# A hybrid transformer block on one core: head norms taken from unscaled products, and six steps of the first head group placed anew

## The chip, the core and the metric

The kernel runs on one core of a Trainium2 chip. The core has five engines with an instruction queue each: PE multiplies matrices and transposes, DVE (vector), ACT (scalar functions) and POOL (general) do element work, and SP issues most of the DMAs. The metric is the device time of one execution in microseconds (us), smaller being better. A difference is told as faster or slower only where it is over 0.2%.

## The reference

One layer of a trunk for 512 tokens of width 1024. A norm and one input projection of 3590 columns give the queries, keys and values of three groups of attention heads of width 64: A (4 heads, two softmax maps a head that are subtracted), B (6 heads, with a running sum of log forget gates) and C (6 heads). Their outputs go through one output projection, then come a gated MLP with a convolution over three tokens and a gated per-layer input. What matters here:

```python
def rms_norm(x, g):
    y = x * lax.rsqrt(jnp.mean(x * x, axis=-1, keepdims=True) + EPS)
    return y * g

hn = rms_norm(h, ln_mix[i])
z = hn @ w_in[i]
(q1, q2, k1, k2, va, qf, kf, vf, fg, qc, kc, vc) = jnp.split(z, IN_SPLITS, axis=-1)
q1 = rms_norm(split_heads(q1, H_DIFF), g[0])      # and so every q and k, per head of 64 columns
```

So a query or key is normed twice: its token's row of 1024 by the layer norm, then its 64 columns by the head norm.

## The kernel before

All matrix products are made of three passes over operands that are split into a high and a low part (`mm3`: high by high, high by low, low by high). The token tiles have 128 tokens, t = 0 to 3. The layer norm's gain is put on the transposed input; its factor per token, a column of `rstd`, isn't multiplied in before the projection, so the products z are unscaled. `token_stats` (L227) makes for a tile the sum of squares on ACT and then three operations of one column on POOL: mean plus EPS (L233), its power -0.5, which is the factor itself (L234), and its square over 64 (L235). The same helper serves the MLP's norm and the last norm, where the fourth column has no reader.

`qk_sums` (L404) squares a tile's 256 query and key columns on ACT, sums each head's 64 squares on DVE, scales the four sums by the fourth column and adds EPS (on DVE for the first pair of heads, on POOL for all others) and raises them to -0.5 on POOL. `qk_scale` (L416) multiplies z by the token's factor and by the head's; its result is called zn. The values are scaled by the token's factor in `in_unit` (L470).

The projection runs pair of heads by pair of heads: A0, A0b (the second map's queries and keys of A0, with the forget gates), A1, A1b, B0 to C2. A part's four token tiles are four slots, each of eight groups of three products (j = 0 to 7), one for each 128 rows of the weight. Slots 0 to 3 hold the first part, written out in `first_products` (L329), where the orders of ACT and DVE are fixed as written; slots 4 to 7 are A0b, 8 to 11 A1, 12 to 15 A1b, 16 to 19 B0, and so on.

The attention of a pair is cut into steps that are laid between the groups. The table `T` (L751) gives for each step its slot and the first group j behind which it may run; `run` (L731) takes one step behind each group, in order of these starts, each step list in its turn, and what is left runs behind the slot's last group. The order on PE is fixed by this. On ACT, DVE, POOL and SP the order of this part is set by a planner that goes by its own estimates of time and by the program's order; `EARLY` (L766) moves some steps forward in it. The steps that matter here:

- `A0a`, `A0b`, `A1a`, `A1b` (`qk_cols`, L505): four transposes of zn for the queries, then four for the keys, each with splits on ACT and DVE and copies of half tiles on POOL, because a head's high and low parts lie in the two halves of the partitions. The queries' tile is named q_p, the keys' k_p. Each takes a bank of PSUM that something before must have left.
- `fc` (`forget_cumsum`, L518), three steps: gates on ACT and DVE; four transposes (pf), a scan on DVE and a DMA of the sums to memory; four transposes back (pq).
- `A0s01`, `A0s02`, `A0s11`, `A0s12` (`scores`, L594): head 0 and head 1, query blocks 0 and 1, or 2 and 3. Each block has two maps; each is two products, a biased minimum on DVE, an exponential on ACT and a reciprocal; POOL scales the second (named with a b, such as A_3b_e) and DVE adds the two. The scores use two PSUM banks in turn. The bias table of a head is made on POOL at its first step, in one of three buffers that `fc` uses too.
- `A0p0`, `A0p1` (`prob_cols`, L618): the transposes of the probabilities, pt and ptc. `A0v0`, `A0v1` (`values`, L646): products of these with the values, po.

Of the kernel before, what the change touches and what calls it, by code (L numbers as in the profile page):

```python
# [12 lines left out]
ALU = mybir.AluOpType  # L13
AX = mybir.AxisListType

P = 128
# [4 lines left out]
HD = 64  # L21
# [3 lines left out]
EPS = 1e-6  # L25
# [56 lines left out]
def kernel(ctx: ExitStack, tc: tile.TileContext, x, xt0, xt, pt_in, small, g_ffn_in, bias_c,  # L82
# [9 lines left out]
    nc = tc.nc  # L92
# [23 lines left out]
    pe, act, dve, pool, sp = (Engine(e) for e in (nc.tensor, nc.scalar, nc.vector, nc.gpsimd, nc.sync))  # L116
# [21 lines left out]
    rstd = cp.tile([P, NT, 4], F32, tag="rstd", name="rstd")  # L138
# [87 lines left out]

    def token_stats(t, src, junk, last=False):  # L227

        r = rstd[:, t, :]
        ins = act.activation(junk, src, AF.Square, accum_out=r[:, 0:1])  # L230
        if last:
            tc.keep_in_program_order(ins)
        nc.gpsimd.tensor_scalar(r[:, 1:2], r[:, 0:1], 1.0 / D, EPS, ALU.mult, ALU.add)  # L233
        nc.gpsimd.tensor_tensor(out=r[:, 2:3], in0=r[:, 1:2], in1=nhalf[:, 0:1], op=ALU.pow)  # L234
        nc.gpsimd.tensor_scalar(r[:, 3:4], r[:, 2:3], r[:, 2:3], 1.0 / HD, ALU.mult, ALU.mult)  # L235

    def split_cols(src, t, g, name, gain=None, tag="t"):

# [69 lines left out]
    for b in range(2):  # L308
        for i in range(2):
            c = HALF[1 - i]  # L310
# [12 lines left out]
    def stats(t):  # L323
        token_stats(t, h[:, t, :], ap.tile([P, D], BF16, tag="e3", bufs=2, name=f"n1_sq{t}"))
        done("n", t)
# [78 lines left out]
    def qk_sums(z, t, name):  # L404
        if name == "A0":
            sq = ap.tile([P, 3 * P], F32, tag="e2", bufs=2, name=f"{name}_sq{t}")[:, : 2 * P]
        else:
            sq = ap.tile([P, 2 * P], F32, tag="sq", bufs=1, name=f"{name}_sq{t}")
        act.activation(sq, z[:, 0 : 2 * P], AF.Square)
        rs = ap.tile([P, 8], F32, tag="rs", bufs=3, name=f"{name}_rs{t}")  # L410
        dve.tensor_reduce(out=rs[:, 0:4], in_=sq.rearrange("p (g c) -> p g c", c=HD), axis=AX.X, op=ALU.add)
        (dve if name in ("A0", "A0b") else pool).tensor_scalar(rs[:, 0:4], rs[:, 0:4], rstd[:, t, 3:4], EPS, ALU.mult, ALU.add)
        pool.tensor_tensor(out=rs[:, 4:8], in0=rs[:, 0:4], in1=nhalf[:, 0:4], op=ALU.pow)
        return rs

    def qk_scale(z, zn, t, rs):  # L416
        dve.scalar_tensor_tensor(zn[:, t, :].rearrange("p (g c) -> p g c", c=HD),
                                       z[:, 0 : 2 * P].rearrange("p (g c) -> p g c", c=HD), rstd[:, t, 2:3],
                                       rs[:, 4:8].unsqueeze(2).broadcast_to([P, 4, HD]), ALU.mult, ALU.mult)

    def feature_cols(zn, j, name):
# [48 lines left out]
    def in_unit(pr, part, n, t, ws, prefetch):  # L470
# [11 lines left out]
        def evac(sums=True, rest=True):  # L482
            if not rest:
                return qk_sums(z, t, name)
            if part == 0:
                v = V[pr]
                vh = bass.AP(v.tensor, v[:, t, :].offset, [v.ap[0], [192, 2], [1, HD]])
                zv = z[:, 2 * P : 3 * P].rearrange("p (g c) -> p g c", c=HD)
                act.activation(vh, zv, AF.Copy, scale=rstd[:, t, 2:3])
                dve.scalar_tensor_tensor(v[:, t, HD : HD + P].rearrange("p (g c) -> p g c", c=HD), zv,  # L490
                                               rstd[:, t, 2:3], f32(vh), ALU.mult, ALU.subtract)
            elif n > 2 * P:
                dve.scalar_tensor_tensor(fg[:, t, 0:6], z[:, 2 * P : 2 * P + 6], rstd[:, t, 2:3], fgb,
                                               ALU.mult, ALU.add)
            return qk_sums(z, t, name) if sums else None

        def evac_done(rs=None):
            qk_scale(z, ZN[pr, part], t, rs or evac())
            done("in", pr, part, t)
# [231 lines left out]
    def run(fill, todo):  # L731
# [17 lines left out]
                pass  # L749

    T = {  # L751
# [112 lines left out]
    for j, (pr, part, *_) in enumerate(PARTS[1:], 1):  # L864
# [7 lines left out]
        for t in range(NT):  # L872
# [3 lines left out]
            if slot >= 37:  # L876
                c = slice((slot - 37) * P, (slot - 36) * P)
# [41 lines left out]
    def ffn_norm(t):  # L919

        token_stats(t, h[:, t, :], mtmp(BF16, 2, f"n2_sq{t}"))
        HN[t] = []
        for g in range(2):
            c = slice(g * S, (g + 1) * S)
            hn = mtmp(F32, 1, f"n2_hn{t}_{g}")
            dve.scalar_tensor_tensor(hn, h[:, t, c], rstd[:, t, 2:3], g_ffn[:, c], ALU.mult, ALU.mult)
            HN[t].append(hn)
# [540 lines left out]
    def first(f, g, a):  # L1468
        def do():
            c = g * NF + f  # L1470
            if a == 0:
                U[c] = bank("zs"[g], f"u{c}")
            cs = slice(a * H, (a + 1) * H)
            for k in range(KD):
                mm3(U[c][:, cs], *first_w[f][1](g, k), Th[k // 4][:, k % 4, cs], Tl[k // 4][:, k % 4, cs], k == 0, k == KD - 1)

        if a == 0:
            us[f, g] = Slot("zs"[g])
        return pe_task(24, do, [first_w[f][0][g], first_w[f][0][2]], FORM if a else (), [us[f, g]] if a == 0 else (), [us[f, g]] if a else ())
# [52 lines left out]
    for f in range(2):  # L1532
        p = [[first(f, g, 1)] for g in range(2)]
# [65 lines left out]
    def stats3(t):  # L1599
        def do():  # L1600
            token_stats(t, h[:, t, :], mtmp(BF16, 2, f"n3_sq{t}"))

        STATS[t] = Task("do", [("act", 1.15)], do, list(H_ADDS.values()), [Slot("conv")])
# [64 lines left out]
    t = 0.0  # L1668
# [122 lines left out]
```

## Time and profile before

| What | Value |
|---|---|
| median of three runs | 725.68 us (725.09 to 725.84) |
| profiled execution, its time | 725.56 us |
| its span | 723.8 us |
| PE busy, products | 706.4 us (98%) |
| PE busy, weight loads | 631.9 us (87%) |
| DVE busy | 536.2 us (74%) |
| ACT busy | 391.8 us (54%) |
| POOL busy | 220.2 us (30%) |
| chain of work that ended last | PE 78%, DVE 10%, DMA 3%, ACT 3%, POOL 2% |

The profile names an instruction by line, engine and operation, then output and inputs. A row of the timeline has its start, its length in us and how many were merged into it, and in brackets how long the engine had been idle before it and what ended that. A row of waits has their total, number and longest. A row of windows gives the stretch, its length, PE's busy time with the number of products, the granted clock as a share of the full one, and the DMA's share and GB/s. A row for one tile gives the count and the shortest, median and longest of an instruction in ns, with the first and last start. Products overlap in a pipeline, so that the length of one is more than the time from one start to the next. The profiler gives nearly all helper instructions the line L108, so one goes by the names of tiles.

### The profile page before, as it was taken

What the parts mean: (1) busy time and instruction counts of PE and PEld (TensorE: products, weight loads), DVE (VectorE), ACT (ScalarE), POOL (GpSimd) and SP (SyncE); (2) the same over time, 40 slices, a digit from 0 to 9 for tenths busy, and PEclk for the clock granted to TensorE, in tenths of its full rate; (3) what the DMA queues carried; (4) which work ended last, traced back from release to release, by engine and by line L of the source; (5) the groups of instructions that cost most, each with busy time, mean ns of one, the idle gap of its engine ahead of it and who ended that gap; (6) DMA issues with size and microseconds to landing.
All of it is one profiled execution on the core that took longest, in us unless ns stands there. A gap on an engine that the chain in (4) does not pass through costs nothing.

```text
span 723.8 us, 11826 instructions
## 1 busy us (share of the span) xinstructions
PE 706.4 (98%) x4182; PEld 631.9 (87%) x4182; DVE 536.2 (74%) x1085; ACT 391.8 (54%) x739; POOL 220.2 (30%) x339
## 2 busy tenths in 40 slices
PE   9898999999999999999999999999999999999997
PEld 8897989988999887889889899988988888999886
DVE  8578787887878854857776998897857677677542
ACT  6646775865766663556354363645434445435721
POOL 4675675766665640200200505100010000000400
PEclk9999999999999999999999999999999999999999
DMA  9444446628414425563844463995595332742441
GB/s 328 176 138 115 123 118 164 204 66 265 131 57 140 146 49 169 161 227 61 190 106 137 96 226 83 242 200 182 167 236 158 94 91 88 234 143 82 156 130 56
DMA packets 43383, 107.35 MB, mean 148 GB/s; under 512 B 4886, under 2 KB 6550, under 8 KB 43324
## 3 DMA queue, kind: packets, MB, share of 16 engines
q1 hardware_dynamic: 38028, 89.51, 38.6%
q0 software_dynamic: 5008, 16.78, 12.8%
q8 instruction: 33, 0.54, 0.3%
q10 hardware_dynamic: 288, 0.30, 0.1%
q14 instruction: 26, 0.21, 0.1%
HBM read 98.31 MB, written 25.18 MB: 171 GB/s over the span
## 4 chain that ended last, share of the span: by engine, by line
PE 78%; DVE 10%; DMA 3%; ACT 3%; POOL 2%; issue 2%; SPq 0%; POOLq 0%; ACTq 0%; DVEq 0%
PE u L108 28%; PE dn_X L108 8%; PE C_z L108 6%; PE pg L108 6%; PE wo L108 5%; PE B_z L108 4%; PE dn_Y L108 4%; PE dn_Z L108 2%; PE A_z L108 2%; DVE w_lo L108 1%; DMA h<-in_x_dram 1%; PE pp L108 1%; PE C_s L108 1%; DVE A_e L108 1%; PE sX L108 1%
## 5 line engine op out<-in xcount | busy, mean ns | idle before, releaser
L108 PE MATMUL u<-Tl,w_hi 128*128 128x512 f32 (+1 forms) x352 | 131.9, 375 | 0.8 <-DVE Tl L108 0.8
L108 PE MATMUL u<-Th,w_hi 128*128 128x512 f32 (+1 forms) x352 | 131.9, 375 | 0.1
L108 PE MATMUL u<-Th,w_lo 128*128 128x512 f32 (+1 forms) x352 | 131.6, 374 | 0.0
L108 ACT CAST w_hi<-w_raw 128x768 fp32r<-128x768 f32 (+1 forms) x116 | 88.6, 786 | 73.2 <-PE u L108 32.4
L108 DVE TENSOR_TENSOR w_lo<-w_raw,w_hi 128x768 fp32r<-128x768 f32 (+1 forms) x116 | 106.5, 933 | 27.5 <-ACT w_hi L108 27.4
L108 DVE SCALAR_TENSOR_TENSOR c<-u,cols,c 128x511 f32<-128x511 f32 x80 | 59.6, 747 | 26.4 <-ACT c L108 25.2
L108 PEld LDWEIGHTS u<-Tl,w_hi 128*128 128x128 f32 x352 | 66.0, 188 | 13.9 <-DVE Tl L108 1.2
L108 PEld LDWEIGHTS u<-Th,w_lo 128*128 128x128 f32 x352 | 66.0, 188 | 13.2
L108 PEld LDWEIGHTS u<-Th,w_hi 128*128 128x128 f32 x352 | 66.0, 188 | 13.1 <-ACT pps L108 0.5
L233 POOL TENSOR_SCALAR rstd<-rstd 128x1 f32<-128x1 f32 x12 | 2.6, 216 | 155.2 <-ACT n_sq L108 154.8
L108 ACT ACTIVATE c<-u,cols 128x512 f32<-128x512 f32 x40 | 31.0, 776 | 29.1 <-PE u L108 29.1
L108 PE MATMUL dn_X<-w_hi,g_ah 128*128 128x256 f32 x144 | 40.6, 282 | 0.4 <-ACT c L108 0.4
L108 PE MATMUL dn_X<-w_hi,g_al 128*128 128x256 f32 x144 | 40.4, 281 | 0.0
L108 PE MATMUL dn_X<-w_lo,g_ah 128*128 128x256 f32 x144 | 40.4, 280 | 0.0
L108 POOL TENSOR_TENSOR w_raw<-w_raw,w_raw 128x768 f32<-128x768 f32 x8 | 15.5, 1938 | 67.1 <-DVE w_lo L108 56.4
L108 PE MATMUL B_z<-B_h,Th 128*128 128x384 f32 x96 | 34.6, 360 | 0.6 <-DVE B_zn L108 0.6
L108 POOL TENSOR_SCALAR tok<-c 128x1 f32<-128x1 f32 x15 | 7.7, 510 | 90.1 <-DVE c L108 90.1
L108 PE MATMUL C_z<-C_h,Th 128*128 128x384 f32 x96 | 34.3, 357 | 0.0
L108 PE MATMUL C_z<-C_h,Tl 128*128 128x384 f32 x96 | 32.3, 337 | 0.0
L108 PE MATMUL B_z<-B_h,Tl 128*128 128x384 f32 x96 | 32.3, 337 | 0.0
L108 PE MATMUL C_z<-C_l,Th 128*128 128x384 f32 x96 | 32.3, 336 | 0.0
L108 PE MATMUL B_z<-B_l,Th 128*128 128x384 f32 x96 | 32.3, 336 | 0.0
(488 smaller groups left out, 2107.0 us busy)
## 6 DMA issues: line engine op xcount, KB each, us to landing
w_raw<-in_w_up_dram SPq DMA_DIRECT2D x44, 384.0 KB, 4.7
w_raw<-in_w_down_dram SPq DMA_DIRECT2D x20, 384.0 KB, 3.6
dsum<-in_w_dsum_dram SPq DMA_DIRECT2D x8, 768.0 KB, 7.0
w_raw<-dsum SPq DMA_DIRECT2D x16, 384.0 KB, 3.7
w_raw<-in_w_up_dram SPq DMA_DIRECT2D x20, 256.0 KB, 4.7
B_r<-in_w_in_dram SPq DMA_DIRECT2D x12, 384.0 KB, 3.4
C_r<-in_w_in_dram SPq DMA_DIRECT2D x12, 384.0 KB, 4.1
wo_r<-in_w_out_dram SPq DMA_DIRECT2D x16, 256.0 KB, 3.0
```

Of the source, the lines that this page charges most:

```text
L108: ins = getattr(self.eng, op)(*a, **k)
L233: nc.gpsimd.tensor_scalar(r[:, 1:2], r[:, 0:1], 1.0 / D, EPS, ALU.mult, ALU.add)
```

## The change

In `token_stats` the fourth column becomes 64 EPS times the mean plus EPS, made from L233's result ahead of the power. In `qk_sums` this is added to the unscaled sum of squares, in place of a product and an addition of EPS. In `qk_scale` the product with the token's factor becomes one with the constant 8, the root of 64. The normed result is the same, since the token's factor cancels: z r / sqrt(r² S / 64 + EPS) = 8 z / sqrt(S + 64 EPS / r²). Six entries of `T` change: A0a goes from group 2 to group 6 of slot 6, fc from 0 to 5 of slot 11, A0s11 and A0s12 from 0 and 1 to 2 and 4 of slot 13, A0v1 from 7 and A1a from 4 to 2 of slot 16.

```diff
@@ token_stats
         nc.gpsimd.tensor_scalar(r[:, 1:2], r[:, 0:1], 1.0 / D, EPS, ALU.mult, ALU.add)
+        nc.gpsimd.tensor_scalar(r[:, 3:4], r[:, 1:2], EPS * HD, None, ALU.mult)
         nc.gpsimd.tensor_tensor(out=r[:, 2:3], in0=r[:, 1:2], in1=nhalf[:, 0:1], op=ALU.pow)
-        nc.gpsimd.tensor_scalar(r[:, 3:4], r[:, 2:3], r[:, 2:3], 1.0 / HD, ALU.mult, ALU.mult)
@@ qk_sums
-        (dve if name in ("A0", "A0b") else pool).tensor_scalar(rs[:, 0:4], rs[:, 0:4], rstd[:, t, 3:4], EPS, ALU.mult, ALU.add)
+        (dve if name in ("A0", "A0b") else pool).tensor_scalar(rs[:, 0:4], rs[:, 0:4], rstd[:, t, 3:4], None, ALU.add)
@@ qk_scale
-                                       z[:, 0 : 2 * P].rearrange("p (g c) -> p g c", c=HD), rstd[:, t, 2:3],
+                                       z[:, 0 : 2 * P].rearrange("p (g c) -> p g c", c=HD), HD ** 0.5,
@@ T
-        "A0a": (6, 2), "A0b": (9, 4), "fc": (11, 0), "A1a": (16, 4), "A1b": (17, 0), "A0s01": (10, 4),
-        "A0s02": (10, 5), "A0p0": (12, 3), "A0s11": (13, 0), "A0v0": (12, 5), "A0s12": (13, 1), "A0p1": (15, 5),
-        "A0v1": (16, 7), "A0n": (17, 0), "A1s01": (18, 2), "A1s02": (18, 5), "A1p0": (20, 5), "A1s11": (20, 6),
+        "A0a": (6, 6), "A0b": (9, 4), "fc": (11, 5), "A1a": (16, 2), "A1b": (17, 0), "A0s01": (10, 4),
+        "A0s02": (10, 5), "A0p0": (12, 3), "A0s11": (13, 2), "A0v0": (12, 5), "A0s12": (13, 4), "A0p1": (15, 5),
+        "A0v1": (16, 2), "A0n": (17, 0), "A1s01": (18, 2), "A1s02": (18, 5), "A1p0": (20, 5), "A1s11": (20, 6),
```

## The prediction

> **What bounds the kernel now.** I read the page's busy times first, then the list of what the matrix engine (PE) waited for, then its rows in order of time around each wait, then the rows of whoever ended the wait.
>
> ```profile
> span 723.8 us, 11826 instructions
> PE 706.4 (98%) x4182; PEld 631.9 (87%) x4182; DVE 536.2 (74%) x1085; ACT 391.8 (54%) x739; POOL 220.2 (30%) x339
> ```
>
> PE is busy for 706.4 of 723.8 us. Nothing in the diff takes a matmul away, so a gain can come only out of the 17.4 us of idle time or out of time at a lower clock. The waits by name:
>
> ```profile
> PE A_q_p L108 <- DVE A_zn L108: 1.9, 2, 1.0
> PE A_pt L108 <- DVE A_e L108: 1.2, 1, 1.2
> ...
> PE A1b_z L108 <- DVE A1b_zn L108: 1.0, 1, 1.0
> ...
> PE pq L108 <- DVE fs L108: 0.9, 1, 0.9
> ...
> PE A_k_p L108 <- DVE A0b_zn L108: 0.6, 1, 0.6
> ```
>
> These five are group A waits, 5.6 us in all, each close to a step that the diff moves. The first and the last are one place, the transposes of the first pair, and the clock falls just behind it (windows of PE, then their granted clock):
>
> ```profile
> 28.90:32.30 3.40, 1.03 (x6) 1.00 0.00 0
> 62.50:65.90 3.40, 2.15 (x19) 1.00 0.85 275
> ```
> ```profile
> 33.00:34.00 1.00, 1.00 (x7) 0.50 0.00 0
> ...
> 35.00:36.00 1.00, 1.00 (x7) 0.53 0.58 174
> 36.00:37.00 1.00, 1.00 (x10) 1.00 0.64 240
> ```
>
> PE worked 1.03 of 3.40 us, and about 3.4 us at half clock followed (0.50, back at 1.00 in the slice from 36). With 2.15 of 3.40 busy, at the A_pt wait, no slice drops.
>
> **A0a four groups later.** In slot 6 it stood behind three of eight groups of three products; it will stand behind seven.
>
> ```profile
> 21.57 0.28 PE L108 MATMUL A0b_z<-A0b_h,Th 128*128 128x262 f32 x1
> ...
> 28.40 0.28 PE L108 MATMUL A0b_z<-A0b_h,Tl 128*128 128x262 f32 x1
> 28.52 0.38 PE L108 MATMUL A_q_p<-ident,A_zn 128*128 128x128 f32 x2
> ...
> 31.10 0.33 PE L108 MATMUL A_q_p<-ident,A_zn 128*128 128x128 f32 x1 [0.95 <-DVE A_zn L108]
> ...
> 32.36 0.94 PE L108 MATMUL A_k_p<-ident,A_zn 128*128 128x128 f32 x4 [0.56 <-DVE A0b_zn L108]
> ...
> 35.72 0.39 PE L108 MATMUL A0b_z<-A0b_h,Th 128*128 128x262 f32 x1
> ```
>
> 57 products from 21.57 to 28.40 give 0.122 us each. Four groups are 12 products, 1.46 us: the q transposes then start at 28.52 + 1.46 = 29.98. The last of them still waits for the fourth A_zn (31.10), and the k transposes for a bank that the first A0b_zn frees (32.36). Neither end moves by much; both are set by DVE and POOL. The k transposes, 0.94 with their drain at half clock, take some 0.4 of PE's time at full clock, so slot 7, which now starts at 35.72, starts at about 32.7: **-3.0 us**. That contains the half clock going away. Idle time becomes 0.8 + 0.56 of a 3.4 us window, some 60% busy, next to the 63% that kept the clock and far from the 30% that lost it. If the clock halves all the same, 3.4 us at half cost 1.7, and the term is -1.3. I take -3.0.
>
> The Trainium skill, "TensorE: Matmul & The Clock Gate", section "What's actually happening", says that the clock halves after an idle window of about 3.4 us. Read strictly, this trace differs, since PE was busy for 1.03 us of the window and lost the clock. By the strict rule the term is -3.0 for certain; by the rows it has the other end of -1.3.
>
> **The norm from unscaled products.** Three POOL operations of one column stay three, but the token's term now comes before the power.
>
> ```profile
> L233 POOL TENSOR_SCALAR rstd<-rstd x4: 190/190/191, 19.4 to 24.7; 128x1 f32<-128x1 f32 x4
> ...
> L235 POOL TENSOR_SCALAR rstd<-rstd x4: 264/264/266, 20.3 to 25.6; 128x1 f32<-128x1 f32 x4
> ```
>
> With a constant in place of a column, L235 should cost what L233 does: 0.07 us less, and the first head norm's power, queued behind it on POOL, gains just that. The add on DVE or POOL and the scaling of the products keep shape and count; their price with one operand fewer isn't shown, bounded by 0 and -0.07 each by the same rows; I take 0, since DVE covers it with other work. The same helper serves the MLP's norm, where the power is what is waited for:
>
> ```profile
> 311.76 0.55 POOL L234 TENSOR_TENSOR rstd<-rstd,nhalf 128x1 f32<-128x1 f32 x1
> ```
> ```profile
> 312.34 1.42 DVE L108 SCALAR_TENSOR_TENSOR n_hn<-h,rstd,g_ffn 128x512 f32<-128x512 f32 x2 [1.49 <-POOL rstd L234]
> ```
> ```profile
> 314.42 0.39 PE L108 MATMUL u<-Tl,w_hi 128*128 128x256 f32 x1 [0.37 <-DVE Tl L108]
> ```
>
> The power starts later by one L233 and its gap, 0.27; DVE runs n_hn and then Tl in that order, and PE already waits 0.37 for Tl: **+0.27**.
>
> **fc to j = 5.** Its four pf transposes, the scan, four pq transposes and the DMA of the running sums go 5 groups later.
>
> ```profile
> 57.18 0.60 PE L108 MATMUL pf<-ident,oall 128*128 128x128 f32 x4
> ...
> 59.22 0.66 PE L108 MATMUL pq<-ident,fs 128*128 128x128 f32 x4 [0.91 <-DVE fs L108]
> ```
>
> Between pf and pq there is still one group, so the 0.9 stays, between 0.7 with DVE free at once and 1.1; I take 0. On SP the loads queued behind the DMA are those of later pairs, wanted slots later: 0. What changes is POOL, where a bias table had to wait for the scan's buffer:
>
> ```profile
> 61.44 1.35 POOL L108 TENSOR_SCALAR bias_A<-oall 128x512 f32<-128x512 f32 x1 [1.08 <-issue]
> 62.89 1.34 POOL L108 TENSOR_SCALAR A_3b_e<-A_3b_e,A_3b_st,nlam 128x512 f32<-128x512 f32 x1
> ```
> ```profile
> 65.49 0.33 PE L108 MATMUL A_pt<-ident,A_e 128*128 128x128 f32 x1 [1.25 <-DVE A_e L108]
> ```
>
> With the scan out of the way the last scores of A0 can be scaled ahead of that table, and A_pt waits no more: **-1.25**. If the order on POOL stays, the table comes up to 2.7 us later (15 products of 384 columns, where 262 take 0.122) and the wait is longer by as much. I take the gain, since the table's buffer would then come free after the scores are ready.
>
> **A0s11 and A0s12 by two and three groups.** The last two of their eight maps go behind the slot's products, so the second A1b tile is complete two maps earlier; its norm is what PE waits for later:
>
> ```profile
> 75.49 0.42 DVE L108 TENSOR_REDUCE A1b_rs<-A1b_sq 128x4 f32<-128x256 f32 x1
> ```
> ```profile
> 78.40 0.36 PE L108 MATMUL A1b_z<-A1b_h,Th 128*128 128x256 f32 x1 [0.98 <-DVE A1b_zn L108]
> ```
>
> **-0.98**, between 0 and that. Two maps back to back wait for a score bank; where that happens now:
>
> ```profile
> 101.27 0.50 PE L108 MATMUL A_s<-A_k_k,A_q_q 128*128 128x512 f32 x1 [0.16 <-DVE A_st L108]
> ```
>
> Two such waits: **+0.35**. The bias table that A0s11 issues on POOL is the one freed by the scan, costed above.
>
> **A1a and A0v1 to j = 2 of slot 16.** A1a runs its two steps first, so it comes two groups sooner, and A0v1 follows at j = 4.
>
> ```profile
> 85.44 0.56 DVE L108 TENSOR_TENSOR ptc<-A_ptc,ptc 128x384 fp32r<-128x384 f32 x1 [0.68 <-ACT ptc L108]
> ```
>
> ```profile
> 88.32 0.64 PE L108 MATMUL A_po<-ptc,A_V 128*128 128x256 f32 x4
> ```
>
> A0v1's last products come two groups, some 1 us, sooner, still after ptc's end at 86.0. No wait stands there to be won: 0, with at most 0.3 lost if ptc slips. A1a's copies on POOL pass the fourth A1b norm, first read a slot later.
>
> **What is late next.** The second pair's transposes come just as its last norm ends:
>
> ```profile
> 35.96 0.23 DVE L108 SCALAR_TENSOR_TENSOR oall<-A0b_z,rstd,fgb 128x6 f32<-128x6 f32 x1 [0.49 <-PE A0b_z L108]
> ...
> 43.50 0.35 DVE L108 SCALAR_TENSOR_TENSOR A_V<-A_z,rstd,A_V 128x128 fp32r<-128x128 f32 x1 [0.95 <-ACT A_V L108]
> ...
> 45.23 0.48 DVE L108 SCALAR_TENSOR_TENSOR A0b_zn<-A0b_z,rstd,A0b_rs 128x256 f32<-128x256 f32 x1 [0.17 <-POOL A0b_rs L108]
> ```
> ```profile
> 45.50 0.60 PE L108 MATMUL A_q_p<-ident,A0b_zn 128*128 128x128 f32 x4
> ```
> ```profile
> L108 DVE TENSOR_TENSOR A1b_l<-A1b_r,A1b_h x3: 681/682/694, 39.5 to 41.3; 128x512 fp32r<-128x512 f32 x3
> ```
>
> PE would be there 3.0 us sooner. DVE has 0.49 + 0.95 + 0.17 = 1.6 us of idle time to give up, which leaves 1.4 of stall; its three A1b splits, 2.0 us, can stand behind, which leaves none. Between 0 and +1.4 I take **+1.0**, nearer the upper end, because DVE still has the first pair's weight splits ahead of all this.
>
> **Sum:** -3.0 - 1.25 - 0.98 + 0.35 + 0.27 + 1.0 = -3.6 us against the profiled execution's 725.56 us (span 723.8 and 1.76 around it; the median of the runs shown is 725.68): 721.9 us.
>
> **Rivals.** *The clock halves all the same*: for it, 60% busy is just under the 63% seen; against it, the 30% that lost the clock is far off. -3.6 + 1.7 = -1.9, 723.7 us.
>
> *POOL keeps its pace, and the gain is given back at the second pair's first map.*
>
> ```profile
> 49.34 1.99 POOL L108 TENSOR_SCALAR A_k_k<-A_k_k 64x512 fp32r<-64x512 f32 x3
> ```
> ```profile
> 51.38 0.39 PE L108 MATMUL A_0b_s<-A_k_k,A_q_q 128*128 128x256 f32 x1
> ```
>
> That map starts 0.05 us after POOL's copies. If they don't come sooner, the 3.0 goes, the 1.0 with it, and the A_pt wait stays: -0.98 + 0.35 + 0.27 = -0.4, 725.2 us. Against it: the copies follow the transposes, which move.
>
> *Slower: the stall moves to the second pair's transposes.* If DVE's order there doesn't change at all and 45.71 stands, PE waits 3.0 us in one piece. This gives back the whole first term, and as that window is then emptier than the one at 28.90, half clock follows, +1.7. The later waits stay too, since DVE is no earlier: -3.0 + 3.0 + 1.7 = +1.7, 727.3 us. It decides once the stall passes about 2 us of a window. Against it: the third A0b tile is now complete before the k transposes, some 4 us sooner, so its sums can run earlier.
>
> **Numbers.** Forecast 0.50, half clock 0.18, given back 0.19, slower 0.13. A run tells 0.2%, 1.45 us, from no change: 724.2 to 727.1. The forecast, most of the second case and a tenth of the third are faster, 0.68; most of the third and small parts of its neighbours are within, 0.21; most of the last is slower, 0.11. The forecast's own range is 720.6 (no stall, no bank waits) to 723.2 (the A_pt wait stays); the wanted one reaches from 719.8, where the 0.9 of pq goes too, to 726.0, and so holds the third case and leaves out the last.
>
> **What would show it.** A0a right: slot 7's products start near 32.7 and no slice from 24 to 45 has a granted clock under 1; wrong: 0.50 again. fc: A_3b_e ahead of the bias table and no A_pt wait. Scores: no A1b_z wait, and short waits for score banks. Norm: a longer wait for Tl near 311. A wait over 2 us of A_q_p for A0b_zn, or of A_0b_s for POOL, would make the prediction wrong.

## The result, and the profile after

The changed kernel takes 721.31 us (median of 5 runs, 720.82 to 723.31), the kernel before 725.68 on the same chip (724.79 to 726.8). The ratio is 0.9946, with an interval from 0.9928 to 0.9965: faster by about 4 us. The profiled execution of the changed kernel took 720.82 us.

```profile
span 718.9 us, 11822 instructions
...
PE 704.3 (98%) x4182; PEld 630.1 (88%) x4182; DVE 534.7 (74%) x1085; ACT 391.2 (54%) x739; POOL 221.6 (31%) x339
```

The span is 4.9 us shorter: 2.1 us of it is PE's busy time, for the same 4182 matmuls, the rest idle time. Of the waits by name (us in total, times, longest), those of group A and of the MLP's start:

```profile
PE A_q_p L108 <- DVE A0b_zn L108: 1.2, 2, 0.7
...
PE pq L108 <- DVE fs L108: 0.9, 1, 0.9
PE A_s L108 <- DVE A_st L108: 0.9, 3, 0.4
PE A_k_p L108 <- DVE oall L108: 0.8, 1, 0.8
PE u L108 <- ACT pps L108: 0.7, 1, 0.7
```

Of the five waits quoted of before, those of A_q_p for A_zn, of A_pt and of A1b_z are gone, and the 0.9 of pq stands. The wait of the k transposes for a bank is still there, with another name: what now frees the bank is the operation that reads the small columns (oall), not the scaling (A0b_zn). New are 1.2 us in front of the **second** pair's q transposes (those of A0b, as in the prediction) and a wait of u for an ACT operation, which was not forecast at all. The two windows of PE around slots 6 to 9 (length, busy, matmuls, granted clock) show the clock at full speed:

```profile
24.00:34.00 10.00, 9.19 (x75) 1.00 0.11 41
34.00:45.00 11.00, 9.78 (x61) 1.00 0.68 193
```

And PE's rows in order of time at the places that the prediction named (start, duration, then in brackets the idle time ahead and who ended it):

```profile
30.13 0.87 PE L108 MATMUL A_q_p<-ident,A_zn 128*128 128x128 f32 x4
...
32.13 0.63 PE L108 MATMUL A_k_p<-ident,A_zn 128*128 128x128 f32 x4 [0.76 <-DVE oall L108]
32.52 0.37 PE L108 MATMUL A0b_z<-A0b_h,Th 128*128 128x262 f32 x1
...
43.23 0.33 PE L108 MATMUL A_q_p<-ident,A0b_zn 128*128 128x128 f32 x1 [0.55 <-DVE A0b_zn L108]
44.23 0.33 PE L108 MATMUL A_q_p<-ident,A0b_zn 128*128 128x128 f32 x1 [0.67 <-DVE A0b_zn L108]
...
60.23 0.66 PE L108 MATMUL pq<-ident,fs 128*128 128x128 f32 x4 [0.93 <-DVE fs L108]
62.14 0.60 PE L108 MATMUL A_pt<-ident,A_e 128*128 128x128 f32 x4
...
70.86 0.50 PE L108 MATMUL A_s<-A_k_k,A_q_q 128*128 128x512 f32 x1 [0.26 <-DVE A_st L108]
```

The q transposes start at 30.13 (29.98 forecast) and slot 7's products at 32.52 (32.7 forecast). The A_pt transposes come without a wait. On POOL the last scaled scores of A0 stand ahead of the bias table, the order that the prediction wanted:

```profile
58.12 1.57 POOL L108 TENSOR_SCALAR A_3b_e<-A_3b_e,A_3b_st,nlam 128x512 f32<-128x512 f32 x1 [1.70 <-DVE A_3b_st L108]
...
60.26 1.25 POOL L108 TENSOR_SCALAR bias_A<-oall 128x512 f32<-128x512 f32 x1 [0.58 <-DVE fs L108]
```

To see where the time went I took the start of one and the same PE instruction in both traces: the first product of slots 7, 12, 13, 14, 15 and 16, one in the middle of group C, one at the MLP's start and the last matmul. Against before, in us:

| start in before | 35.72 (slot 7) | 62.33 (12) | 69.04 (13) | 74.42 (14) | 78.40 (15) | 82.35 (16) | 199.06 (C) | 317.89 (MLP) | 718.44 (last) |
|---|---|---|---|---|---|---|---|---|---|
| after | -3.20 | -1.69 | -3.08 | -2.45 | -3.59 | -3.30 | -3.51 | -4.21 | -4.87 |
| step from the column before | -3.20 | +1.51 | -1.39 | +0.63 | -1.14 | +0.29 | -0.21 | -0.70 | -0.66 |
| the forecast's term | -3.0 | +1.0 | -1.25 | +0.35 | -0.98 | 0 | 0 | +0.27 | 0 |

Term by term this looks like the forecast with one wrong sign. It isn't quite: the experiments below time the parts by themselves, and a single trace turns out to hold 0.6 us and more that belong to the run and not to the kernel.

### The profile page after: what moved, and what is told of

Read it like the earlier page. It is cut to its first block, busy times and chain, and to the rows that moved or that the text cites. A ratio compares the mean times of both kernels' runs of the same rounds, so it can differ in the third digit from the quotient of the medians.

```text
span 718.9 us, 11822 instructions
## 1 busy us (share of the span) xinstructions
PE 704.3 (98%) x4182; PEld 630.1 (88%) x4182; DVE 534.7 (74%) x1085; ACT 391.2 (54%) x739; POOL 221.6 (31%) x339
## 4 chain that ended last, share of the span: by engine, by line
PE 82%; DVE 6%; DMA 4%; ACT 3%; POOL 2%; issue 2%; SPq 0%; POOLq 0%; ACTq 0%; DVEq 0%
PE u L108 31%; PE dn_X L108 9%; PE C_z L108 6%; PE pg L108 6%; PE dn_Y L108 4%; PE wo L108 4%; PE B_z L108 4%; PE dn_Z L108 2%; PE A1b_z L108 1%; DMA waq<-in_w_in_dram 1%; PE sX L108 1%; DMA h<-in_x_dram 1%; PE C_s L108 1%; PE B_s L108 1%; DMA wo_l<-wo_r 1%
```

## The experiments

Each was timed against the kernel before on the same chip. Ratios are to before, with their intervals; before was at 725.1 to 725.7 in all of them. "Against after" compares medians and traces of two kernels.

**The norm alone, and the moved steps alone.** Two kernels split the change: one has the diff's norm with the old table of steps, the other the old norm with the new table.

```
norm_only:   the change's token_stats, qk_sums, qk_scale; T as before
steps_only:  those three as before; T as in the change
```

> The new norm with the old step table. Theory (the norm gains in two places): the first pair's fourth norm ends some 0.6 us sooner, so the first wait of 1.9 us falls by about that and the clock still halves behind it, and the MLP's start is 0.6 us shorter because the planner orders it anew; the A_pt wait (1.25), the A1b_z wait (0.98) and the pq wait (0.9) stay. Time about 1.2 us under the kernel before, 724.5. Rival (the steps do it all, the norm only costs 0.27 in the MLP's norm, as was predicted): 725.6 to 726.

> The new step table with the old norm. Theory: the idle time at the first pair's transposes is some 0.6 us more than with both, no half clock, no A_pt and no A1b_z wait, the MLP's start as before: about 3.5 us under the kernel before, 722.2. Rival (without the shorter norm the window at the first pair is empty enough that the clock halves again, 1.7 us more): 723.9.

Measured: norm_only 724.27 us (12 runs), ratio 0.9979, from 0.9970 to 0.9987; steps_only 723.99 (11 runs), 0.9977, from 0.9967 to 0.9987. So the norm is worth about 1.5 us, where the prediction's terms gave a loss of 0.2, and the steps about 1.7 us, where they gave 3.9. The right total was made of two wrong halves. Together they bring 3.9 by the ratio (2.5 to 5.2); the two alone add up to 3.2.

steps_only comes out at the time of its rival, 723.9, but not by the rival's cause: its trace has full clock from 24 to 45 us. Where its steps fall short can be read from the starts that the table uses. Against before, slot 7 is 2.51 us sooner, the way from there to slot 12 gives back 2.26 (forecast +1.0), and slot 13 loses 1.55 (forecast +0.35), with a wait of 0.62 for a score bank; slots 12 and 14 bring 1.39 and 1.14, near the forecast's 1.25 and 0.98. norm_only's trace is of its slowest run (726.16 us), so its gain can't be read from its starts.

Where the norm's gain lies early shows in the scaling itself (tile view: shortest, median and longest ns, first and last start). First after, then before:

```profile
L108 DVE SCALAR_TENSOR_TENSOR A_zn<-A_z,A_rs x4: 417/424/424, 26.7 to 30.2; 128x256 f32<-128x256 f32 x4
```
```profile
L108 DVE SCALAR_TENSOR_TENSOR A_zn<-A_z,rstd,A_rs x4: 482/484/485, 27.0 to 30.6; 128x256 f32<-128x256 f32 x4
```

With a constant in place of a column the same scaling takes 0.06 us less, each time. The chain is timed from the square of the last token tile, whose last row on ACT is, after and before:

```profile
24.26 0.19 ACT L108 ACTIVATION_READ_ACCUMULATOR n_sq<-h 128x1 f32 x1
```
```profile
24.38 0.19 ACT L108 ACTIVATION_READ_ACCUMULATOR n_sq<-h 128x1 f32 x1
```

From there to the last A_zn (30.20 and 30.56 to two places) it is 5.94 us after and 6.18 before; norm_only has 5.94 and steps_only 6.19. So the new norm shortens this chain by 0.24 us, not by 0.07. (Where that square came early, at 23.58 to 23.86 in three of the experiments, something else set the last A_zn: 6.45 to 6.73.)

**The token's term after the power.** The norm's other place is the start of the MLP, where the prediction had +0.27 and the table shows -0.70. DVE's rows there, after:

```profile
308.51 0.69 DVE L108 TENSOR_TENSOR Tl<-n_t,Th 128x512 fp32r<-128x512 f32 x1 [1.05 <-ACT Th L108]
309.25 1.41 DVE L108 SCALAR_TENSOR_TENSOR n_hn<-h,rstd,g_ffn 128x512 f32<-128x512 f32 x2
310.58 0.68 DVE L108 TENSOR_TENSOR Tl<-n_t,Th 128x512 fp32r<-128x512 f32 x1
```
```profile
310.76 0.39 PE L108 MATMUL u<-Th,w_hi 128*128 128x256 f32 x1 [0.73 <-ACT pps L108]
```

Before, n_hn (312.34) came ahead of Tl, and PE waited for two Tl. Now the planner, which puts DVE's work in an order by costs and due times, has the power ready later and fills DVE's time with Tl first. To test that cause, this kernel changes only the order of two POOL instructions, for every token:

```
     nc.gpsimd.tensor_scalar(r[:, 1:2], r[:, 0:1], 1.0 / D, EPS, ALU.mult, ALU.add)
-    nc.gpsimd.tensor_scalar(r[:, 3:4], r[:, 1:2], EPS * HD, None, ALU.mult)
     nc.gpsimd.tensor_tensor(out=r[:, 2:3], in0=r[:, 1:2], in1=nhalf[:, 0:1], op=ALU.pow)
+    nc.gpsimd.tensor_scalar(r[:, 3:4], r[:, 1:2], EPS * HD, None, ALU.mult)
```

> The changed kernel with the power ahead of the token's term again (same formula). The order on PE is the same. Theory (the later power made the planner put two splits of the MLP's start ahead of the norm, and that is where the 0.6 us at the MLP's start come from): the two waits for Tl return and PE is some 0.6 us later from there, while the first pair is up to 0.2 us later: 721.9. Rival (the prediction's step, that the later power costs 0.27 at the MLP's start): PE is 0.27 us sooner there, 721.1.

Measured: 723.21 us (6 runs), 0.9962, from 0.9950 to 0.9974. Its list of waits has the old one again:

```profile
PE u L108 <- DVE Tl L108: 0.8, 2, 0.4
```

Against after it is 1.45 us later in the middle of C and 2.03 at the MLP: 0.58 us is lost between the two, where the orders of DVE and ACT at the MLP's start are the only difference from after on PE, DVE and ACT. In the ten traces that have the new order there, this stretch is 0.52 to 1.06 us shorter than in before; in the three others, with the old order, it lies between 0.12 shorter and 0.40 longer. So that much of the norm's gain is shown to be the planner's new order. For the first 1.45 the traces show no such cause: up to the MLP the orders of PE, DVE and ACT are those of after, and POOL's differs in the exchanged operations alone. In this run A1b's raw weights landed later (3.9 us from issue, median, 3.3 after), the waits for the second pair's transposes were longer (1.8, not 1.2), and slot 13 had two waits for score banks where after has one. But the six runs have a median 1.9 us above after's (1.2 by the ratios, whose intervals overlap), so whether a part of the 1.45 is the kernel's stays open.

**A0a alone, and the change without A0a.**

```
a0a_alone:  before, with "A0a": (6, 6)
a0a_back:   after, with "A0a": (6, 2)
```

> The kernel before with A0a alone moved to group 6. The prediction's largest term: -3.0 at the first pair and 1.0 given back at the second, 2.0 us faster, 723.6. Theory from the runs so far (the fourth norm of the second pair, not PE, sets when slot 9 goes on; it follows the fourth norm of the first pair by 13.6 to 14.1 us whether A0a is early or late): slot 7 starts over 2 us sooner and the second pair's wait eats nearly all of it, 0.5 us faster, 725.1.

> The changed kernel with A0a back at group 2 of slot 6. Theory (the gain at A0a, 3.2 us at the start of slot 7, is partly given back at the second pair's transposes, 1.65 us): the half clock behind the first transposes returns, the A_q_p wait for A0b_zn is gone, and the kernel is 1.5 us slower than the changed one, 722.9. Rival (the later wait at the second pair was not caused by the earlier PE): that wait stays and the kernel is 3.2 us slower, 724.5.

Measured: a0a_alone 724.82 us (11 runs), 0.9995, from 0.9986 to 1.0004, no change; a0a_back 722.09 (5 runs), 0.9948, from 0.9936 to 0.9961, not told from after; in its trace the A_q_p wait for A0b_zn is down to 0.3 us. Alone, the step with the largest term of the sum is worth nothing that could be told from noise. Its trace says where the gain went. Waits, then PE's rows, of a0a_alone:

```profile
PE A_q_p L108 <- DVE A0b_zn L108: 2.3, 2, 1.6
```
```profile
44.45 0.33 PE L108 MATMUL A_q_p<-ident,A0b_zn 128*128 128x128 f32 x1 [1.62 <-DVE A0b_zn L108]
...
46.13 0.60 PE L108 MATMUL A_k_p<-ident,A0b_zn 128*128 128x128 f32 x4
```

and the k transposes of before:

```profile
46.47 0.60 PE L108 MATMUL A_k_p<-ident,A0b_zn 128*128 128x128 f32 x4
```

PE comes to slot 7 3.06 us sooner, waits 2.3 us in front of the second pair's transposes, and has the k transposes only 0.34 us sooner. From slot 12 to the MLP's start a0a_alone is 0.37 to 0.31 us ahead. What sets this place is not PE but the last A0b_zn, and that hardly moved: 45.23 before, 44.89 here. What the half clock costs is a question of its own. First the windows of a0a_back, which has A0a's old place, then one of norm_only, which has it too:

```profile
24.00:34.00 10.00, 8.23 (x65) 1.00 0.14 53
34.00:45.00 11.00, 10.71 (x72) 1.00 0.73 209
```
```profile
34.00:45.00 11.00, 11.00 (x68) 0.87 0.61 198
```

With the same place of A0a the clock fell in one execution and not in the other. But PE was busier in the latter: its emptiest 3.4 us there (from 29.00) hold 1.63 us of work, those of norm_only (from 29.50) 1.02. The window nearest to the prediction's 1.03 that kept its clock is that of a0a_alone in front of the second pair:

```profile
42.20:45.60 3.40, 1.13 (x8) 1.00 0.91 244
```

No slice from there to 50 us drops. The runs of before, 49 in these comparisons, say what it costs. 3.4 us at half clock take 0.002 off the mean granted clock of a run, and the idle end of the span takes up to as much (fc_back's trace has a mean of 0.998 and full clock up to 715 us). So a mean of 0.999 and more excludes such a stretch, and one of 0.997 and less points to it, though its place is not on record. The 20 runs of the first kind have a median of 725.4 us, the 22 of the second 725.6; on the two chips with many of both they stand 0.5 and 0.2 apart. So the half clock comes and goes by run and by this comparison costs 0.2 to 0.5 us, not 1.7; the likely reason is that the same late A0b_zn covers it. In the kernels with the new place it isn't excluded either: two of the 11 runs of a0a_alone have 0.996 and 0.997 and take 1.6 us more than its median, and the changed kernel's slowest run (723.31 us) has 0.997. No trace shows it there.

**What holds the second pair's chain.** The rows behind the wait, in the changed kernel: ACT's, then DVE's.

```profile
37.74 1.27 ACT L108 CAST A1b_h<-A1b_r 128x512 fp32r<-128x512 f32 x2 [1.38 <-DMA A1b_r<-in_w_in_dram]
38.92 0.38 ACT L108 ACTIVATE A0b_sq<-A0b_z 128x256 f32<-128x256 f32 x1
```
```profile
38.49 2.12 DVE L108 TENSOR_TENSOR A1b_l<-A1b_r,A1b_h 128x512 fp32r<-128x512 f32 x2
...
43.75 0.42 DVE L108 SCALAR_TENSOR_TENSOR A0b_zn<-A0b_z,A0b_rs 128x256 f32<-128x256 f32 x1 [0.25 <-POOL A0b_rs L108]
```

ACT stands idle for 1.38 us until raw weights of A1b land, casts two tiles of them (1.27) and only then squares the fourth A0b tile; DVE spends 2.12 us on the same weights. They are used from slot 12. Two kernels put this weight work behind steps of the fourth A0b tile's norm: one only the casts on ACT, the other the work of all three engines.

```
 casts_behind:
+        if name == "A0b" and t == NT - 1:          # in qk_sums, after the square
+            X["sq"] = act.last
+        if j == 2:                                 # in load_next
+            with tc.issue_after(X["sq"]):
+                nxt.append(f())
+            return
 splits_behind: the same, behind three instructions of that tile:
                its square (ACT), its addition (DVE), its power (POOL)
```

> The changed kernel with the four A1b weight casts behind the square of the fourth A0b tile on ACT. Theory (the second pair's stall, 1.2 us in the changed kernel's profile and 1.8 in another of the same order, is set by the landing of the A1b weights, since a cast that waits for them stands on ACT ahead of that square): the A_q_p wait for A0b_zn falls under 0.4 us, and the kernel is 1 to 1.5 us faster than the changed one, 720.1. Rival (the stall is DVE's work, as the prediction priced it): the wait stays over 1 us, 721.3.

> The changed kernel with the A1b weight work behind the second pair's fourth sums on all three engines: the casts behind the square on ACT, the splits behind the addition on DVE, the accumulating DMA behind the power on POOL. Theory (the second pair's chain is late because this work, not needed until slot 12, stands ahead of it): the A_q_p wait for A0b_zn is under 0.3 us; 1 us faster than the changed kernel, 720.3. Rival (the chain is long by its own operations): the wait stays near 0.9, 721.3.

Measured: casts_behind 721.61 us (6 runs), 0.9949, from 0.9936 to 0.9962: nothing against after. The square came sooner, 6.93 us behind the fourth A_zn and not 8.72, but a wait of 0.9 stayed, since the next two engines of the chain took up the weights in its place. DVE's rows, then POOL's:

```profile
40.95 1.48 DVE L108 TENSOR_TENSOR A1b_l<-A1b_r,A1b_h 128x512 fp32r<-128x512 f32 x2
42.36 0.22 DVE L108 TENSOR_SCALAR A0b_rs<-A0b_rs,rstd 128x4 f32<-128x4 f32 x1
```
```profile
42.67 0.98 POOL L172 DMA_DIRECT2D A1b_l<-A1b_r  x1
43.36 1.36 POOL L108 TENSOR_TENSOR A0b_rs<-A0b_rs,nhalf 128x4 f32<-128x4 f32 x1
```

splits_behind: 721.23 us (5 runs), 0.9936, from 0.9923 to 0.9950. From the fourth A_zn to the fourth A0b_zn it takes 12.26 us (13.55 after, 14.67 before), and the wait of A_q_p for A0b_zn is gone from the list altogether:

```profile
PE pq L108 <- DVE fs L108: 0.9, 1, 0.9
PE A_s L108 <- DVE A_st L108: 0.9, 3, 0.3
...
PE A_k_p L108 <- DVE oall L108: 0.8, 1, 0.8
```

So the cause of the changed kernel's wait is shown: A1b's weight work in front of the second pair's norm. No run moves that work in a0a_alone; there it is the likely cause, with the weights landing 4.3 us from issue (median), 3.1 in before. But slot 12, 0.81 us ahead of after, is followed by slot 14 at 0.21 ahead: 0.6 comes back in slot 13, with two waits for score banks where after has one:

```profile
69.04 0.45 PE L108 MATMUL A_s<-A_k_k,A_q_q 128*128 128x384 f32 x1 [0.31 <-DVE A_st L108]
...
70.66 0.50 PE L108 MATMUL A_s<-A_k_k,A_q_q 128*128 128x512 f32 x1 [0.30 <-DVE A_st L108]
```

and the times of splits_behind and after aren't told apart. With the chain out of the way, does A0a's place count?

```
splits_behind_a0a_back:  splits_behind, with "A0a": (6, 2)
```

> The same with A0a back at group 2 of slot 6. Theory (with the second pair's chain out of the way, PE is the bound there, so that A0a's place counts in full): 1.5 us slower than with A0a at group 6, 721.8, no A_q_p wait for A0b_zn. Rival (A0a's place is hidden by something else still): the same time, 720.3.

Measured: 722.59 us (5 runs), 0.9955, from 0.9943 to 0.9968. Against splits_behind it is 1.60 us later at slot 7, 1.06 at slot 12 and 1.36 by the medians, with intervals that just overlap. Before, the same step brought 0.4, and 0.8 by the medians in the changed kernel (a0a_back). This is what one expects if the chain covered the step's gain, and by these intervals it is likely, not certain.

**fc back to its place.**

```
fc_back:  after, with "fc": (11, 0)
```

> The changed kernel with fc back at group 0 of slot 11. Theory (the scan held up the last scores of A0 behind a bias table on POOL): the A_pt wait of 1.2 us returns, pq still waits 0.9, 722.5. Rival (the A_pt wait went because of the other moves): no A_pt wait, 721.3.

Measured: 723.10 us (5 runs), 0.9970, from 0.9958 to 0.9982; 1.8 above after by the medians. POOL's order and PE's wait are those of before again:

```profile
59.95 1.35 POOL L108 TENSOR_SCALAR bias_A<-oall 128x512 f32<-128x512 f32 x1 [1.09 <-issue]
61.40 1.34 POOL L108 TENSOR_SCALAR A_3b_e<-A_3b_e,A_3b_st,nlam 128x512 f32<-128x512 f32 x1
```
```profile
64.00 0.33 PE L108 MATMUL A_pt<-ident,A_e 128*128 128x128 f32 x1 [1.25 <-DVE A_e L108]
```

At slot 12 it is 0.20 us behind after, at slot 13 1.59: the term of 1.25 and its cause are right.

**The scan's own wait.** The 0.9 of pq stayed, as forecast. This kernel tries to fill it with one more group of products:

```
 splits_behind_fc_gap: splits_behind, with "fc": (11, 4), and in fc
                       one more yield between the scan and the pq transposes
```

> The same with A0a at group 6, and fc from group 4 with one group more between its pf and pq transposes. Theory (pq waits for the scan for as long as one group is short of it): the pq wait falls from 0.9 to 0.4, 719.8. Rival (the scan then starts later, behind other work of DVE): it stays 0.9, 720.3.

Measured: 720.91 us (5 runs), 0.9935, from 0.9923 to 0.9948, the same as splits_behind. PE's rows, then DVE's:

```profile
56.67 0.60 PE L108 MATMUL pf<-ident,oall 128*128 128x128 f32 x4
...
59.24 0.66 PE L108 MATMUL pq<-ident,fs 128*128 128x128 f32 x4 [0.92 <-DVE fs L108]
```
```profile
57.09 0.96 DVE L108 TENSOR_TENSOR B_l<-B_r,B_h 128x768 fp32r<-128x768 f32 x1
57.97 1.22 DVE L108 TENSOR_TENSOR_SCAN fs<-f_ones,pf 128x512 f32<-128x512 f32 x1
```

The pf transposes come 0.69 us sooner than in splits_behind, but the scan only 0.17: in both it stands right behind a weight split of group B on DVE. So the wait is DVE's order, not PE's distance. This kernel has the lowest median of all, 0.4 us under after, which these intervals don't tell from it.

**The maps, and slot 16, back.**

```
maps_back:    after, with "A0s11": (13, 0), "A0s12": (13, 1)
slot16_back:  after, with "A1a": (16, 4), "A0v1": (16, 7)
```

> The changed kernel with A0s11 and A0s12 back at groups 0 and 1 of slot 13. Theory (the two maps behind the slot let the second A1b norm come sooner): the A1b_z wait of 1.0 us returns, and the 0.6 us that slot 13 is longer by go, so 0.4 us slower, 721.7. Rival (the A1b_z wait went because DVE is ahead of its work anyway): no A1b_z wait, and 0.6 us faster, 720.7.

> The changed kernel with A1a back at group 4 and A0v1 back at group 7 of slot 16. Theory (as predicted, no wait stands there, so the two moves are worth nothing): the same within 0.3 us, 721.3. Rival (they start A0's last norm and A1's splits sooner, which later steps of DVE need): waits behind slot 17 grow, 722.3.

Measured: maps_back 722.51 us (6 runs), 0.9962, from 0.9949 to 0.9975, 1.2 above after by the medians. Two waits are there that the changed kernel doesn't have:

```profile
70.96 0.44 PE L108 MATMUL A_2b_s<-A_k_k,A_q_q 128*128 128x384 f32 x1 [0.67 <-DVE A_1b_st L108]
...
77.00 0.36 PE L108 MATMUL A1b_z<-A1b_h,Th 128*128 128x256 f32 x1 [0.96 <-DVE A1b_zn L108]
```

Slot 13 isn't shorter with the old places, as the theory had it, but 0.32 us longer than in after, and from slot 13 to 16 the kernel loses 1.13 us against it. slot16_back: 722.02 us (5 runs), 0.9957, from 0.9945 to 0.9969. By the medians that is 0.7 above after, not told apart; in the traces slot 16, where the two differ, starts 0.62 us behind and ends 0.59 behind, so what it lost came before its own difference: 0.68 of it in slot 13, with two waits for score banks where after has one, though up to slot 16 the order of work is the same on PE, DVE, ACT and POOL.

## Why the prediction was right, and where it wasn't

The time was forecast at 721.9 and is 721.31. The steps, in their order:

- **A0a four groups later, -3.0.** Slot 7 starts where it was forecast, at full clock, and the mechanism on PE is right. The worth isn't: the step alone is worth 0.4 us by its ratio, from a gain of 1.0 to a loss of 0.3.
- **What is late next, +1.0.** This is the term that failed. The prediction asked how much idle time DVE could give up in front of the last A0b_zn, and put the weight splits behind it. In the changed kernel's trace its size is near (1.2 us of wait, 1.51 up to slot 12), but not by the mechanism, and in the trace of A0a alone 2.7 of the 3.06 us come back, 2.3 of it as one pair of waits. What stood in front was the work on A1b's raw weights: the wait of ACT's queue for their landing, the casts, DVE's splits, and POOL's accumulating DMA. The prediction saw the splits on DVE and looked at none of ACT's rows, where the chain begins with the square. A rival named this place, with 3.0 of stall, a clock lost and a slower kernel. Its place was right, but with 2.3 us of wait a0a_alone's trace kept the clock, and the kernel wasn't slower. In the changed kernel 1.2 remain, with A_zn 0.24 sooner by the new norm and the weights landing 1.0 us sooner (median) than in the trace of a0a_alone. The prediction also names the first pair's weight splits as standing ahead; these rows (A_l) are those of A1.
- **The half clock, 1.7.** The rate was right (0.50), the price wrong: in slots 7 and 8 PE isn't what sets the end, and by the comparison of runs half clock costs 0.2 to 0.5. The Trainium skill, "TensorE: Matmul & The Clock Gate", section "What's actually happening", says that the window of the clock gate is free-running. That agrees with what these runs show, runs of before that had such a stretch by their mean clock and runs that had none, and windows of nearly the same work (1.03 and 1.13 us of 3.40) that lost and kept it. It also means that the rival could not have been decided from one trace.
- **The norm, -0.07 and 0 early, +0.27 at the MLP.** Wrong in both parts, and together worth 1.5. Early, the scaling's 0.06 per tile was inside the bounds, but it was taken as covered; the chain from the last token's square to the last A_zn, which PE waits for, got 0.24 shorter. At the MLP the step "DVE runs n_hn and then Tl in that order" failed: a power that is ready later made the planner choose another order, and 0.58 of gain came in place of a loss. Some 0.7 us of the 1.5 is not accounted for; the planner also gave DVE and POOL other orders in group A.
- **fc, -1.25.** Right in size, place and cause, and the 0.9 of pq stayed as forecast.
- **The maps, -0.98 and +0.35.** The mechanism is right: the A1b_z wait is gone and short waits for score banks came. The second term was too small: slot 13 is longer by 0.63 in the changed kernel's trace and by 0.52 to 1.55 in the ten traces with the new places (two waits of 0.16, which the prediction rests on, would be 0.32). The old places cost 1.13 in the trace.
- **Slot 16, 0.** Nothing is seen there in the traces.
- **POOL keeps its pace** (rival). Not so: A0a's gain is lost before POOL's copies, and A_pt's wait is gone.

The forecast was right since the steps' shortfall, about 2.2 of 3.9, and the norm's gain, about 1.7 more than forecast, nearly cancel; so the right total is in good part luck. Two things stay open: where the rest of the norm's gain lies, and why the changed kernel's trace gains 0.66 us behind the MLP's start. 0.39 of that is a wait of dn_X for an ACT operation at 426.9 us, which before has and after hasn't; the gain is complete by 655 us, ahead of the last norm, the only code behind the MLP's start that the change touches. Against before the same stretch stands anywhere from -0.65 (maps_back) to +0.38 (splits_behind) in the experiments' traces, so it is likely the run's.

## What to carry to other kernels

Before you credit a step that brings an engine sooner to its next wait, follow that wait back over every engine of its chain, and ask of each what stands in its queue ahead of the link: here weights for a stage that starts over 20 us later stood in three queues, and moving them out of one only showed them in the next. Where a planner orders the work, a cost that moves by some 0.3 us can change the order, so a term that rests on "in that order" needs the other order as a bound. Time the halves of a change apart: a right total says little of its terms.

## What the runs showed of the hardware

- DVE's scaling of 128x256 with a tensor and a second factor takes 402 to 425 ns with a constant as that factor (eleven traces) and 475 to 485 with a column of 128 values (three traces).
- Half clock after a thin stretch isn't fixed to the kernel: PE busy 1.03 of 3.40 us (before) and 1.02 (norm_only) lost the clock, 1.13 (a0a_alone) and 1.63 (a0a_back) kept it, and of 49 runs of before 22 had a mean granted clock of 0.997 and less, 20 one of 0.999 and more, 0.2 to 0.5 us apart in the median.
- Two traces with the same order of work on PE, DVE, ACT and POOL up to slot 16 (after and slot16_back) stood 0.63 us apart there. Two that differ before the MLP in the order of two small POOL operations a tile (after and power_first) stood 1.45 us apart in the middle of group C, with a landing of the same weights that differed by 0.6 us in the median. The last row of the fourth token tile's square started anywhere from 23.58 to 25.82 us in the fourteen traces. So under about 1 us a term can't be read from a difference of two traces' starts; the waits by name and the medians of runs decide.
